# Smaller first transfers on two queues, GpSimd squares with a fold, and one load issued one tile earlier, in a hybrid decoder layer on one core

## The chip, the cores and the metric

The kernel runs on one core of a Trainium2 chip. The metric is the time of one execution on the device, in microseconds (us). The core has five engines that run side by side and wait for each other through semaphores: TensorE (PE; its weight loads are shown apart as PEld), VectorE (DVE), ScalarE (ACT), GpSimd (POOL) and SyncE (SP). SyncE here does nothing but issue transfers between the main memory and the on-chip memory (SBUF); ScalarE's queue may issue transfers too. TensorE writes to the accumulator banks (PSUM).

## What is computed

A decoder layer for 1024 tokens of width 1024 in float32. The change touches the first and the third of these steps:

```python
h = rmsnorm(x, ln1[l])
z = h @ w_in[l]
...
x = x + jnp.concatenate([ml_out, fx_out], axis=-1) @ w_out[l]
x = x + cross_attention(rmsnorm(x, ln_x[l]), rmsnorm(mem, ln_mem[l]), w_xq[l], w_xkv[l], w_xo[l])
u = jax.nn.relu(rmsnorm(x, ln2[l]) @ w_ff1[l])
x = x + (u * u) @ w_ff2[l]
return rmsnorm(x, ln_f)
```

Here `rmsnorm(x, g)` is `x * rsqrt(mean(x*x) + eps) * g` over the width, and between the second and third line stand an mLSTM group and a forgetting-attention group of heads, whose outputs are concatenated.

## The kernel before

**Layout.** Activations lie with the width on the 128 partitions: x is 8 tiles (k = 0 to 7) of 128 x 1024 tokens, kept as two halves (hf = 0, 1) of 512 tokens, `xs[hf][k]`, in the buffers `xa` and `xb`. Every matmul is done in three passes over operands split into a high part (`wh`, or `act` for activations) and a low part (`wl`): `mm3`, L184 to L186. `split` makes the two parts: ScalarE copies the high part (L132, or L135 with a scale), VectorE subtracts it to get the low part (L133, or L136 with a scale).

**The opening.** The first product is that of the mLSTM values with 16 gate columns beside them, 272 columns in all. L323 to L332 issue its transfers: for each k the tile of x (L319), for every even k the weights of two k (L326), and on ScalarE's queue the vector of gains and biases (`vec`, L329) and the gate weights (L330). In the block `with in_order()` (L377) the order of each compute engine is that of the program text: for each k the weights are split (`cut_w`), the gate weights of three k at k = 0, 2, 4 (`cut_gates`), the tile of x is scaled by its gain and split (`cut_x`), and twelve matmuls follow (`first_values`, four token tiles of three passes). A second loop does the same for hf = 1 with three token tiles. The normalisation is applied to the results, so the sum of squares is only needed then: `square_to` (L363) squares two tiles at once into `wide`, 128 x 1024 with tile k-1 in the left half and tile k in the right; `add_to` (L366) adds these on VectorE; `rsqrt_sums` (L238) sums over the partitions with matmuls against a column of ones, two parts (left and right) for each of four token tiles; L196, GpSimd's power (L202) and L207 to L209 turn the sums into the factors `rcol`, and `first_sink` uses them (L311, L375). The sums of hf = 0 are taken at k = 1 of the second loop, and the three VectorE operations that follow them stand in VectorE's order ahead of `cut_x(1, 6)`. The sums of hf = 1 come later, outside the block (L416).

**The rest of the order.** Outside such blocks a scheduler that models the engines orders the instructions, and transfers go out on SP's queue in its order.

**The second output projection.** The heads' outputs lie in main memory as `mix`. The projection is done in two parts; the second (`out_proj`, loop at L1069 over hf) takes its operands from `mix_load` (L845, two transfers of 768 KB for each hf, high and low part). Those for hf = 0 are loaded ahead of the loop, those for hf = 1 inside `full_sink` (L1073), held behind the store `done` (L1078) of one of the tiles n of hf = 0. `full_sink` loads the partial sum of the first projection (L1076), adds (L1077), stores, splits (L135, L136) and squares (L226, L230). The weights of this projection come by L172.

Of the kernel before, what the change touches and what calls it, by code (L numbers as in the profile page):

```python
# [11 lines left out]
AF = mybir.ActivationFunctionType  # L12
ALU = mybir.AluOpType
# [6 lines left out]
TH = 512  # L20
# [24 lines left out]
def hybrid_layer(ctx: ExitStack, tc: tile.TileContext, a: dict, out: bass.AP):  # L45
    nc = tc.nc
    v, s, g = nc.vector, nc.scalar, nc.gpsimd
# [7 lines left out]
    def name(tag):  # L55
        count[0] += 1
        return f"{tag}_{count[0]}"
# [4 lines left out]
    def act(dt=F32R):  # L62
        return sb("act", [P, 8, TH], 7, dt)
# [8 lines left out]
    def w4(shape=(P, 1024), dt=F32):  # L72
        t = sb("w4", [P, 1024], 5, dt)[: shape[0]]
        return t.rearrange("p (a b) -> p a b", b=shape[2]) if len(shape) == 3 else t

    def z4():
        return sb("z4", [P, T + 3], 2)

    def w2(tag, n=512, dt=F32, p=P):
        return sb("r_" + tag, [P, 512], BUFS[tag], dt)[:p, :n]  # L80
# [6 lines left out]
    def ps_tile(tag):  # L87
        return psum.tile([P, 512], F32, tag=tag, name=name(tag), bufs=PBUFS[tag])
# [19 lines left out]
    def const(n, shape, dt=F32):  # L108
        return pool.tile(shape, dt, tag=n, name=n, bufs=1)

    load = nc.sync.dma_start
# [29 lines left out]
    @contextmanager  # L141
    def in_order():

        traced = nc.cur_bb.bb.instructions
        last = traced[-1]
        yield
        start = next(k for k in reversed(range(len(traced))) if traced[k] is last) + 1
        for i in traced[start:]:
            if i.engine not in COMPUTE:
                continue  # L150
            if i.engine in last_of:
                tc.add_manual_dep(
                    i,
                    last_of[i.engine],
                    mybir.DependencyInfo(mybir.DependencyClass.NoSync, mybir.DependencyReason.DATA),
                    reason="in_order",
                )
            last_of[i.engine] = i.name


    def rotate(*tags):

        spare[tags] = spare.get(tags, -1) + 1
        return w2(tags[spare[tags] % len(tags)])
# [58 lines left out]
    def square_sum(acc, x, first, by=s, add=v):  # L223
        sq = acc if first else w2("c")[:, : x.shape[-1]]
        if by is s:
            s.activation(sq, x, AF.Square)  # L226
        else:
            by.tensor_tensor(out=sq, in0=x, in1=x, op=ALU.mult)
        if not first:
            add.tensor_tensor(out=acc, in0=sq, in1=acc, op=ALU.add)  # L230

    def rsqrt_sums(acc, r, nt, parts=1, bank=None, over=None, how=rsqrt_cols):

        ps = (bank or ov_)()
        for t in range(nt):
            for e in range(parts):
                at = (e * nt + t) * P
                nc.tensor.matmul(ps[:, t : t + 1], acc[:, at : at + P], ones, start=e == 0, stop=e == parts - 1)  # L238
        return how(r, ps[:, :nt], 1.0 / D, nt, over)
# [13 lines left out]
    rcol = const("rcol", [P, 8])  # L253
# [47 lines left out]
    xs = [[t[:, k] for k in range(KT)] for t in (xa, xb)]  # L301
# [11 lines left out]
    def load_x(hf, i):  # L313
        for k in range(4 * i, 4 * i + 4):
            load(xs[hf][k], a["x"][:, k, hf * TH : hf * TH + TH])
# [5 lines left out]
    raws = [sb("wr", [P, 1024], 2) for _ in range(2)]  # L321
    wg_raw = z4()[:, : KT * 16].rearrange("p (k c) -> p k c", k=KT)
    for k in range(KT):  # L323
        if k % 2 == 0:
            c = slice(k % 4 * 256, k % 4 * 256 + 512)
            load(raws[k // 4][:, c], a["w_mv"][0, k // 4, :, c])  # L326
        load_x(0, k)
        if k == 0:
            s.dma_start(vec, a["vec"])  # L329
            s.dma_start(wg_raw, a["w_gate"])  # L330
    for k in range(KT):
        load_x(1, k)  # L332

# [6 lines left out]
    def cut_x(hf, k, n=1):  # L340
        for c in range(0, TH, TH // n):
            c = slice(c, c + TH // n)
            split(h[hf][0][:, k, c], h[hf][1][:, k, c], xs[hf][k][:, c], vec[:, VEC["ln1"] + k :][:, 0:1])

    def first_values(hf, k, ts):
        w = both(ws[k // 3], lambda z: z[:, k % 3])
        for t in ts:
            mm3(tiles[hf][t], both(h[hf], lambda z: z[:, k, t * P : (t + 1) * P]), w, k == 0, k == KT - 1)

    def cut_w(k):  # L350
        w = both(ws[k // 3], lambda z: z[:, k % 3, :256])
        split(*w, raws[k // 4][:, k % 4 * 256 : k % 4 * 256 + 256])

    def cut_gates(i):
        w = both(ws[i], lambda z: z[:, :, 256:])
        split(*w, wg_raw[:, 3 * i : min(3 * i + 3, KT)])


    wide = [w4() for _ in range(3)]
    pairs_ = lambda hf, k: (xa, xb)[hf][:, k - 1 : k + 1].rearrange("p a b -> p (a b)")  # L360

    def square_to(t, hf, k):
        s.activation(t, pairs_(hf, k), AF.Square)  # L363

    def add_to(t, u):
        return v.tensor_tensor(out=t, in0=t, in1=u, op=ALU.add)  # L366
# [5 lines left out]
    def first_sink(hf, t):  # L372
        ps = tiles[hf][t]
        mv_sink(4 * hf + t, 0, ps[:, :256])
        v.tensor_scalar(out=z[:, 4 * hf + t], in0=ps[:, 256:], scalar1=rcol[:, 4 * hf + t : 4 * hf + t + 1], scalar2=None, op0=ALU.mult)  # L375

    with in_order():  # L377
        for k in range(KT):
            cut_w(k)
            if k in (0, 2, 4):  # L380
                cut_gates(k // 2)
            cut_x(0, k, 1 if k else 2)
            if k in (1, 3, 5):
                square_to(wide[k // 2], 0, k)
            if k == 4:
                add_to(wide[0], wide[1])
            first_values(0, k, range(4))
        square_to(wide[1], 0, 7)
        cut_x(1, 0)
        add_to(wide[0], wide[2])  # L390
        cut_x(1, 1)
        add_to(wide[0], wide[1])
        for k in range(2, 6):
            cut_x(1, k)
        for k in range(KT):
            if k in (2, 3):
                cut_x(1, k + 4)
            if k == 2:
                square_to(wide[1], 1, 1)
            if k == 4:  # L400
                square_to(wide[2], 1, 3)
            first_values(1, k, range(3))
            if k == 1:
                rsqrt_sums(wide[0], rcol[:, 0:4], 4, 2)
            if 2 < k < 7:
                first_sink(0, k - 3)
            if k == 6:
                add_to(wide[1], wide[2])
                square_to(wide[0], 1, 5)
        square_to(wide[2], 1, 7)  # L410
        add_to(wide[1], wide[0])
        last_sum = add_to(wide[1], wide[2])
    tiles[1].append(ps_tile("mm")[:, :WV])
    for k in range(KT):
        first_values(1, k, (3,))
    rsqrt_sums(wide[1], rcol[:, 4:8], 4, 2)  # L416
    for t in range(4):
        first_sink(1, t)

# [264 lines left out]
    for _ in range(2):  # L684
        t = act().rearrange("p a b -> p (a b)").rearrange("p (i c) -> p i c", i=4)
# [156 lines left out]
    def mix_load(k0, k1, hf):  # L842
        t = act().rearrange("p (e k) c -> p e k c", e=2)
        for p_ in range(2):
            load(t[:, p_, : k1 - k0].bitcast(F32), mix[hf, p_, :, k0:k1])  # L845
        return [(t[:, 0, k], t[:, 1, k]) for k in range(k1 - k0)]
# [204 lines left out]
    n = 0  # L1051
# [7 lines left out]
    for step in fill:  # L1059
        n, e = divmod(halves[0], 2)  # L1060
# [8 lines left out]
    for hf in range(2):  # L1069
        hi, lo = act(), act()  # L1070
        acc = w2("b")

        def full_sink(n, hf, ps):  # L1073
            t = rotate("p", "d", "e")
            with tc.issue_after(last_raw[0].ins):
                load(t, x1d[hf, :, n])  # L1076
            v.tensor_tensor(out=t, in0=ps, in1=t, op=ALU.add)  # L1077
            done = load(x1d[hf, :, n], t)  # L1078
            if hf == 0 and n == 1:
                with tc.issue_after(done.ins):  # L1080
                    mix_fx.append(mix_load(MLH + KX, KT, 1))
            split(hi[:, n], lo[:, n], t, vec[:, VEC["ln_x"] + n :][:, 0:1])
            square_sum(acc, t, n == 0)
            if hf == 1 and n == KT - 3:
                mix_done.append(done)
            if hf and n == 2:
                rsqrt_sums(acc0, rcol[:, 0:4], 4)
            if hf and n == 4:
                row_second(0)

        def row_second(hf):
            at = slice(hf * TH, hf * TH + TH)
            to_row(row[:, at], rcol[:, 4 * hf : 4 * hf + 4], 4, rowd[2:3, at])

        out_proj(a["w_out_b"], mix_fx[hf], hf, full_sink)
        h2.append((hi, lo))
        acc0 = acc
# [197 lines left out]
    for n in range(KT):  # L1295
# [7 lines left out]
        k = n % 4  # L1303
# [150 lines left out]
    for at, (p_, i) in enumerate(jobs):  # L1454
# [19 lines left out]
        b, k = todo[p_][:2]  # L1474
# [53 lines left out]
    for at, (b, m) in enumerate(steps):  # L1528
# [14 lines left out]
        x = x2[m // 2][:, m % 2]  # L1543
# [16 lines left out]
    for i in range(2):  # L1560
        t = act()
# [122 lines left out]
```

## Time and profile before

| | us |
|---|---|
| median of 3 runs | 1526.88 |
| lowest and highest | 1526.77, 1527.15 |
| the profiled execution, its own time | 1527.38 |
| its span, from the first to the last instruction | 1525.5 |
| TensorE busy in it | 1504.9 |
| VectorE busy | 1103.9 |
| ScalarE busy | 722.6 |
| GpSimd busy | 444.7 |
| first matmul begins | 6.46 |

The profile is one execution seen by the hardware profiler; times in it count from the first instruction. A row of the timeline has the start, the duration (of a group, from its first start to its last end), engine, line, operation, output and inputs by the program's names, shapes, count, and in brackets how long the engine stood idle before it and what ended that. A row of a group of instructions has, behind the count, the busy time and the mean duration in ns. Rows with "q" (SPq, ACTq) are instructions that issue transfers. A row "A <- B: total, times, longest" says how long A waited for B.

### The profile page before, as it was taken

The page shows a single profiled execution, that of the slowest core. Times are in us where ns is not written, and L with a number is a line of the kernel's source. Part 1 is how long each engine was busy: PE and PEld are TensorE (multiplying, and loading weights), DVE is VectorE, ACT ScalarE, POOL GpSimd, SP SyncE. Part 2 cuts the span into 40 slices and gives each one's busy share as a digit, 9 for nine tenths or more (in the row PEclk, how much of TensorE's full clock was granted, in tenths as well). Part 3 has the DMA queues.
Part 4 walks back from the last instruction along what each step waited for, and adds up shares of the span by engine and source line. Part 5 has one row for each costly group of instructions (what it writes and reads, how often), then busy time and mean ns, then how long its engine had stood idle before and what let it go on. Part 6 is the DMA issues. An engine that isn't in the chain of part 4 may idle for free.

```text
span 1525.5 us, 21947 instructions
## 1 busy us (share of the span) xinstructions
PE 1504.9 (99%) x7729; PEld 1261.5 (83%) x7729; DVE 1103.9 (72%) x1740; ACT 722.6 (47%) x1353; POOL 444.7 (29%) x498
## 2 busy tenths in 40 slices
PE   8999999999999999999999999999999999999997
PEld 8988888889899888788888888888888888888887
DVE  7675676764788885854557888887987788777765
ACT  7333343434688763644444456655566432222134
POOL 1003030413455441001100033433343644343312
PEclk9999999999999999999999999999999999999998
DMA  6232323435887957953334436777775975555623
GB/s 240 80 107 77 124 77 124 132 127 158 262 246 226 297 189 272 320 202 118 124 133 161 169 104 242 283 268 249 261 263 207 365 262 221 220 221 219 250 83 111
DMA packets 118075, 297.24 MB, mean 195 GB/s; under 512 B 13119, under 2 KB 27769, under 8 KB 111821
## 3 DMA queue, kind: packets, MB, share of 16 engines
q1 hardware_dynamic: 117676, 295.73, 56.4%
q8 instruction: 61, 1.00, 0.3%
q14 instruction: 50, 0.40, 0.1%
q10 hardware_dynamic: 288, 0.11, 0.0%
HBM read 199.08 MB, written 96.71 MB: 194 GB/s over the span
## 4 chain that ended last, share of the span: by engine, by line
PE 94%; DMA 2%; DVE 1%; ACT 1%; issue 1%; POOL 0%; SPq 0%; DVEq 0%; ACTq 0%; POOLq 0%
PE tp L184 8%; PE tp L186 8%; PE tp L185 8%; PE sc L184 6%; PE sc L186 6%; PE sc L185 6%; PE m L184 6%; PE mm L184 6%; PE m L186 6%; PE m L185 6%; PE mm L186 6%; PE mm L185 6%; PE ov L785 2%; PE ov L184 2%; PE ov L185 2%; PE ov L186 2%
## 5 line engine op out<-in xcount | busy, mean ns | idle before, releaser
L185 PE MATMUL tp<-act,wh 128*128 128x512 f32 (+1 forms) x456 | 178.7, 392 | 1.3 <-DMA act<-mix 1.3
L184 PE MATMUL tp<-act,wl 128*128 128x512 f32 (+1 forms) x456 | 179.2, 394 | 0.6 <-DVE wl L133 0.4
L186 PE MATMUL tp<-act,wh 128*128 128x512 f32 (+1 forms) x456 | 178.4, 392 | 0.0
L132 ACT ACTIVATE wh<-wr 128x1024 fp32r<-128x1024 f32 (+3 forms) x100 | 96.1, 962 | 107.6 <-PE tp L186 36.6
L133 DVE TENSOR_TENSOR wl<-wr,wh 128x1024 fp32r<-128x1024 f32 (+3 forms) x100 | 116.9, 1170 | 21.1 <-ACT wh L132 21.0
L184 PE MATMUL mm<-act,wl 128*128 128x512 f32 (+1 forms) x332 | 128.3, 386 | 0.0
L185 PE MATMUL mm<-act,wh 128*128 128x512 f32 (+1 forms) x332 | 126.9, 382 | 0.0
L186 PE MATMUL mm<-act,wh 128*128 128x512 f32 (+1 forms) x332 | 126.8, 382 | 0.0
L184 PE MATMUL m<-act,wl 128*128 128x512 f32 (+1 forms) x308 | 119.5, 388 | 0.0
L186 PE MATMUL m<-act,wh 128*128 128x512 f32 (+1 forms) x308 | 117.7, 382 | 0.0
L185 PE MATMUL m<-act,wh 128*128 128x512 f32 (+1 forms) x308 | 117.6, 382 | 0.0
L185 PEld LDWEIGHTS tp<-act,wh 128*128 128x128 f32 x456 | 85.8, 188 | 20.7 <-issue 1.6
L184 PEld LDWEIGHTS tp<-act,wl 128*128 128x128 f32 x456 | 85.8, 188 | 20.4 <-DVE wl L133 0.8
L186 PEld LDWEIGHTS tp<-act,wh 128*128 128x128 f32 x456 | 85.8, 188 | 19.6
L184 PE MATMUL sc<-act,wl 128*128 128x512 f32 (+1 forms) x260 | 100.8, 388 | 0.0
L185 PE MATMUL sc<-act,wh 128*128 128x512 f32 (+1 forms) x260 | 100.5, 387 | 0.0
L186 PE MATMUL sc<-act,wh 128*128 128x512 f32 (+1 forms) x260 | 100.5, 387 | 0.0
L1428 POOL TENSOR_TENSOR z<-wr 128x256 f32<-128x256 f32 x56 | 54.8, 998 | 143.6 <-DMA wr<-w_ff2q 130.3
L132 ACT ACTIVATE w<-wr 128x768 fp32r<-128x768 f32 (+2 forms) x31 | 25.5, 825 | 131.7 <-PE tp L186 69.6
L132 ACT ACTIVATE wh<-z 128x1024 fp32r<-128x1024 f32 (+2 forms) x55 | 52.5, 956 | 64.5 <-POOL z L1428 28.3
L133 DVE TENSOR_TENSOR wl<-z,wh 128x1024 fp32r<-128x1024 f32 (+2 forms) x55 | 68.2, 1240 | 9.9 <-ACT wh L132 9.9
L186 PEld LDWEIGHTS mm<-act,wh 128*128 128x128 f32 x332 | 62.4, 188 | 12.6
(657 smaller groups left out, 4205.7 us busy)
## 6 DMA issues: line engine op xcount, KB each, us to landing
act<-right SPq DMA_DIRECT2D x35, 1024.0 KB
right<-r_d SPq DMA_DIRECT2D x70, 256.0 KB
right<-w SPq DMA_DIRECT2D x56, 256.0 KB
wr<-w_ff2q SPq DMA_DIRECT2D x28, 512.0 KB
act<-fqk SPq DMA_DIRECT2D x48, 256.0 KB
wr<-w_in SPq DMA_DIRECT2D x20, 512.0 KB
wr<-w_ff SPq DMA_DIRECT2D x20, 512.0 KB
fqk<-r_p SPq DMA_DIRECT2D x32, 256.0 KB
```

The lines of the kernel that those rows point to most:

```text
L132: s.activation(hi, src, AF.Copy)
L133: return v.tensor_tensor(out=lo, in0=src, in1=hi.bitcast(F32), op=ALU.subtract)
L184: nc.tensor.matmul(ps, w[1], x[0], start=first, stop=False, skip_group_check=more)
L185: nc.tensor.matmul(ps, w[0], x[1], start=False, stop=False, skip_group_check=more)
L186: nc.tensor.matmul(ps, w[0], x[0], start=False, stop=last, skip_group_check=more)
L785: nc.tensor.matmul(self.ov[:, c0:], self.fv[:, self.j], t[:, c0:], start=self.j == 0 and t is self.p[1], stop=self.last and t is self.p[0])
L1428: g.tensor_tensor(out=o, in0=x, in1=y, op=op)
```

## The change

Three edits.

First, the opening's first transfers are cut into pieces of 128 KB: the weights of k = 0 and of k = 1 are loaded apart, the left half of x's first tile goes on ScalarE's queue in place of the gate weights, and SP issues the weights of k = 0, the gate weights, the right half of that tile, and then the rest as before.

Second, the squares of hf = 0 (four of 128 x 1024) are multiplications on GpSimd and no longer squares on ScalarE. After the last addition of each half GpSimd adds the right half of `wide` onto the left (`fold`, 128 x 512), and `rsqrt_sums` takes one part for each token tile where it took two.

Third, the load of the operands of hf = 1 stands behind the store of tile n = 0, where it stood behind that of n = 1.

```diff
     for k in range(KT):
-        if k % 2 == 0:
-            c = slice(k % 4 * 256, k % 4 * 256 + 512)
+        if k < 2 or k % 2 == 0:
+            c = slice(k % 4 * 256, k % 4 * 256 + (512 if k > 1 else 256))
             load(raws[k // 4][:, c], a["w_mv"][0, k // 4, :, c])
-        load_x(0, k)
-        if k == 0:
+        if k:
+            load_x(0, k)
+        else:
+
             s.dma_start(vec, a["vec"])
-            s.dma_start(wg_raw, a["w_gate"])
+            s.dma_start(xs[0][0][:, :256], a["x"][:, 0, :256])
+            load(wg_raw, a["w_gate"])
+            load(xs[0][0][:, 256:], a["x"][:, 0, 256:512])
...
     def square_to(t, hf, k):
-        s.activation(t, pairs_(hf, k), AF.Square)
+        x = pairs_(hf, k)
+        if hf:
+            s.activation(t, x, AF.Square)
+        else:
+            g.tensor_tensor(out=t, in0=x, in1=x, op=ALU.mult)
+
+    def fold(t):
+
+        g.tensor_tensor(out=t[:, :TH], in0=t[:, :TH], in1=t[:, TH:], op=ALU.add)
...
         add_to(wide[0], wide[1])
+        fold(wide[0])
...
-                rsqrt_sums(wide[0], rcol[:, 0:4], 4, 2)
+                rsqrt_sums(wide[0], rcol[:, 0:4], 4)
...
         last_sum = add_to(wide[1], wide[2])
+        fold(wide[1])
...
-    rsqrt_sums(wide[1], rcol[:, 4:8], 4, 2)
+    rsqrt_sums(wide[1], rcol[:, 4:8], 4)
...
-            if hf == 0 and n == 1:
+            if hf == 0 and n == 0:
                 with tc.issue_after(done.ins):
                     mix_fx.append(mix_load(MLH + KX, KT, 1))
```

GpSimd's order in the opening, from the setting up of constants on (`c_y` is the output of the power, L202; `w` are the buffers of `wide`). Before:

```order
L124 AFFINE_SELECT causal<-causal 128x128
L498 MEMSET z_71_788 128x3
L202 TENSOR_TENSOR c_y_320<-c_var_318,half 128x4
L440 MEMSET w_40_476 12x1024
L202 TENSOR_TENSOR c_y_439<-c_var_437,half 128x4
```

And of the change (its lines are 14 higher behind the new functions; L371 is the square, L375 the fold):

```order
L124 AFFINE_SELECT causal<-causal 128x128
L371 TENSOR_TENSOR w_25_134<-act_86 128x1024
L371 TENSOR_TENSOR w_26_135<-act_86 128x1024
L371 TENSOR_TENSOR w_27_136<-act_86 128x1024
L512 MEMSET z_71_784 128x3
L371 TENSOR_TENSOR w_26_135<-act_86 128x1024
L375 TENSOR_TENSOR w_25_134<-w_25_134 128x512
L202 TENSOR_TENSOR c_y_319<-c_var_317,half 128x4
L454 MEMSET w_40_472 12x1024
L375 TENSOR_TENSOR w_26_135<-w_26_135 128x512
L202 TENSOR_TENSOR c_y_435<-c_var_433,half 128x4
```

Four squares and a fold now stand ahead of the first power, and a second fold ahead of the second.

SP's queue at the second output projection: the stores of the tiles of hf = 0 (`x1d<-r_p`, `r_e`, `r_d`: the tiles n = 0, 2, 1 in the scheduler's order), the loads of partial sums (`<-x1d`) and the operands (`<-mix`). Before:

```order
L1076 DMA r_p_6950<-x1d 128x512
L1078 DMA x1d<-r_p_6886 128x512
L1078 DMA x1d<-r_e_6931 128x512
L1076 DMA r_p_7019<-x1d 128x512
L1078 DMA x1d<-r_d_6903 128x512
L845 DMA act_6907<-mix 128x1536 x2
L1078 DMA x1d<-r_p_6950 128x512
L1076 DMA r_e_7066<-x1d 128x512
L172 DMA wr_7092<-w_out_b 128x768
```

And of the change:

```order
L1090 DMA r_p_6946<-x1d 128x512
L1092 DMA x1d<-r_p_6882 128x512
L859 DMA act_6886<-mix 128x1536 x2
L1092 DMA x1d<-r_e_6927 128x512
L1090 DMA r_p_7015<-x1d 128x512
L1092 DMA x1d<-r_d_6902 128x512
L1092 DMA x1d<-r_p_6946 128x512
L172 DMA wr_7088<-w_out_b 128x768
L1090 DMA r_e_7062<-x1d 128x512
```

The two loads of operands stand three places further ahead, directly behind the store of tile 0, and two stores and one load now follow them.

## The prediction

> **What bounds the kernel now.** I read the page first, then the waits of TensorE, then the stretches in which it waits.
>
> ```profile
> span 1525.5 us, 21947 instructions
> PE 94%; DMA 2%; DVE 1%; ACT 1%; issue 1%; POOL 0%; SPq 0%; DVEq 0%; ACTq 0%; POOLq 0%
> ...
> PE mm L184 <- DVE act L136: 6.5, 1, 6.5
> PE tp L185 <- DMA act<-mix: 1.3, 1, 1.3
> PE tp L184 <- DVE wl L133: 0.4, 1, 0.4
> ```
>
> The chain that ended last is TensorE for 94% of the span, so only what makes TensorE wait, or takes an instruction from it, can change the time. The change works at two of its waits: the 6.5 us ahead of the first matmul, and the wait for `act<-mix` near 624 us. It also takes column sums from TensorE and gives GpSimd work in the opening. So I looked at the opening by stretches (columns: length, then busy time and count of PE, PEld, DVE, ACT, POOL, then clock, DMA share, GB/s).
>
> ```profile
> 6.46:10.70 4.24, 4.24 (x18) 4.24 (x19) 3.44 (x8) 4.24 (x9) 0.00 (x0) 1.00 1.01 383
> 10.70:16.00 5.30, 5.30 (x43) 5.30 (x43) 4.67 (x10) 5.30 (x12) 0.10 (x1) 1.00 1.05 392
> 16.00:20.00 4.00, 4.00 (x34) 4.00 (x33) 3.60 (x7) 4.00 (x7) 0.00 (x0) 1.00 1.05 399
> 20.00:25.00 5.00, 5.00 (x44) 5.00 (x43) 5.00 (x8) 5.00 (x10) 0.00 (x0) 1.00 0.43 161
> ```
>
> TensorE runs without a gap from 6.46 on: 18 matmuls in 4.24 us (0.236 each), then 43 in 5.30 (0.123). VectorE is nearly full beside it: 3.44 + 4.67 + 3.60 + 5.00 = 16.71 us busy of 18.54, so 1.83 us of it are free. GpSimd does nothing. The two engines meet at the seventh tile of the second half (k = 6), where VectorE's cut (L136) at 28.53 releases the matmul at 29.33, after a gap of about 0.2:
>
> ```profile
> 28.53 1.41 DVE L136 SCALAR_TENSOR_TENSOR act<-act,vec,act 128x512 fp32r<-128x512 f32 x2
> ...
> 28.99 0.29 PE L186 MATMUL sc<-wh,act 128*128 128x272 f32 x1
> 29.33 0.39 PE L184 MATMUL sc<-w,act 128*128 128x272 f32 x1
> ```
>
> So VectorE has no slack there: what delays it before 28.5 delays TensorE.
>
> **First transfers.** Before, SP issues 256 KB of weights and then 256 KB of x, and ScalarE the vectors and gate weights:
>
> ```profile
> 0.79 0.40 SPq L326 DMA_DIRECT2D wr<-w_mv  x1
> 1.20 0.45 ACTq L330 DMA_DIRECT2D z<-w_gate  x1
> 1.25 0.91 SPq L319 DMA_DIRECT2D act<-x  x2
> ...
> 4.47 0.42 ACT L132 ACTIVATE wh<-wr 128x256 fp32r<-128x256 f32 x1 [1.50 <-DMA wr<-w_mv]
> 5.38 0.91 ACT L135 ACTIVATE act<-act,vec 128x256 fp32r<-128x256 f32 x2 [0.15 <-DMA act<-x]
> ```
>
> The first matmul needs 128 KB of each; now only these stand ahead, on two queues, so 256 KB fewer. At the 383 GB/s of the second stretch that is 0.67 us; nothing at least, 1.0 at most if the weights' earlier arrival counts too. I take 0.7: first matmul near 5.7. The bytes up to x's second tile are the same, so that tile comes no sooner (an estimate: 5.38 plus 256 KB at 383 GB/s, so about 6.0).
>
> **Squares on GpSimd.** Four squares of 128x1024 leave ScalarE and become GpSimd operations with two SBUF inputs. No such size is in the trace. The nearest rows:
>
> ```profile
> L1172 POOL TENSOR_TENSOR r_e<-z,z 128x512 f32<-128x512 f32 x7 | 9.1, 1298 | 130.6 <-DMA z<-w_ff 127.9 <-DVE w L1172 2.7
> L230 POOL TENSOR_TENSOR r_b<-r_c,r_b 128x256 f32<-128x256 f32 x10 | 7.3, 734 | 32.7 <-ACT r_c L226 32.7
> L751 POOL TENSOR_SCALAR w<-w,c_den 128x512 f32<-128x512 f32 x8 | 5.5, 693 | 11.1 <-DVE c_den L748 5.3 <-ACT r_c L794 1.9 <-ACT wh L952 1.8
> ```
>
> 256 more elements cost 1.298 - 0.734 = 0.564 us, so 1024 take 1.298 + 2 x 0.564 = 2.43; I take 2.4. Upper end 2 x 1.298 = 2.6; lower end 2 x 0.693 = 1.39, if squaring one tensor reads it once, as the one-input form does. (The Trainium skill, GPSIMD Engine Reference, section 3.1, gives 4497 ns for an add of 2048 elements; halved, an estimate of 2.25, with which the sum below would be 0.7 us lower. No run here shows that size.)
>
> The price is not GpSimd's own time but VectorE's. Rows of both engines, elsewhere in the kernel:
>
> ```profile
> 906.10 1.30 POOL L1172 TENSOR_TENSOR z<-z,z 128x512 f32<-128x512 f32 x1
> 907.37 1.75 POOL L1172 TENSOR_TENSOR r_e<-wr,wr 128x512 f32<-128x512 f32 x1
> 909.20 2.16 POOL L1211 TENSOR_TENSOR wr<-wr 128x512 f32<-128x512 f32 x1
> ...
> 906.84 1.12 DVE L1172 TENSOR_TENSOR w<-r_f,r_p 128x512 f32<-128x512 f32 x1 [0.17 <-ACT r_f L1326]
> 907.88 2.32 DVE L133 TENSOR_TENSOR wl<-z,wh 128x1024 fp32r<-128x1024 f32 x1
> ...
> L505 DVE SCALAR_TENSOR_TENSOR z<-z,vec,z x24: 1270/1277/1857, 78.6 to 320.4; 128x1024 f32<-128x1024 f32 x24
> ...
> 18.09 1.22 DVE L366 TENSOR_TENSOR w<-w,w 128x1024 f32<-128x1024 f32 x1
> 19.23 0.74 DVE L136 SCALAR_TENSOR_TENSOR act<-act,vec,act 128x512 fp32r<-128x512 f32 x1
> ```
>
> L1172 on VectorE ends at 907.96, which is GpSimd's end (907.40) plus its own 0.6. GpSimd's next takes 1.75 instead of 1.30: it waited for that end. L133, begun at 907.88, takes 2.32 where 1.22 is usual, so it started at GpSimd's end, 909.12; GpSimd's next then takes 2.16. The two take turns, whole instructions at a time; the form with a scalar does so too (L505, 1.857 against 1.27). Every operation of VectorE in the opening has two SBUF inputs.
>
> I walk through the opening by turns, with VectorE's steps (start to start; its rows overlap by 0.08, as 18.09 + 1.22 and 19.23 show): an addition 1.14, a cut of 512 0.66, a weight split 0.34.
>
> ```profile
> 6.72 0.42 DVE L133 TENSOR_TENSOR wl<-wr,wh 128x256 fp32r<-128x256 f32 x1
> ...
> 21.03 2.73 DVE L136 SCALAR_TENSOR_TENSOR act<-act,vec,act 128x512 fp32r<-128x512 f32 x4
> ```
>
> The first square starts when x's second tile is there (6.0) and VectorE has ended its split of weight 1 (6.72 + 0.34 before, now 0.7 sooner), so at 6.3, and holds VectorE to 8.7. Cut 1 runs, 8.7 to 9.4. Tile 3, three loads of 256 KB behind tile 1, has meanwhile landed (6.0 + 3 x 0.67 = 8.0, the ninth microsecond at the latest): second square 9.4 to 11.8. One weight split, then the third square, 12.1 to 14.5. Only now comes cut 2 (14.6 to 15.3): TensorE, done with k=1 at 11.2, waits about 4.2 us. Weight splits and cuts 3 and 4 follow, then the addition of the first two squares; the fourth square needs that addition (18.9 to 21.3), and k=5 waits 2.2 us. Then the rest of VectorE's list, into which the fold puts one more turn (28.2 to 29.5, 1.3). The cut of 28.53 comes at 36.5: **8.0 us later**. Check by sums: 4 x 2.4 + 1.3 = 10.9 of turns, less the 1.83 free, less 0.7 that VectorE starts sooner, is 8.4. That ScalarE is rid of four squares is no gain: it was ahead of VectorE by then. The last wait before that cut is GpSimd's power (L202) behind the sums, as before. TensorE passes that point 8.0 us later, and the first transfers' 0.7 is spent in its waits. At 1.39 a square (and 0.69 the fold) the same count gives 4 x 1.39 + 0.69 - 1.83 - 0.7 = 3.7; at 2.6 it gives 9.2, 0.8 more.
>
> **Fewer sums.** The fold halves the column sums of L238:
>
> ```profile
> 40.84 1.84 PE L238 MATMUL ov<-ones,w 128*128 128x1 f32 x16
> 42.55 0.36 PE L184 MATMUL m<-wh,act 128*128 128x256 f32 x1
> ```
>
> Sixteen pass in 1.71 us, so eight save 0.86. The first set lies ahead of the late cut and saves nothing; the second saves 0.86. Its fold has cover: TensorE has matmuls of its list to do meanwhile, and the sums stand 13 of them later in the new order. Without cover it would cost its 1.3.
>
> **The second projection's operands.** They are issued at 617.88, behind the store of tile 1; now behind that of tile 0, whose store went out at 612.85, so about 4.6 us sooner.
>
> ```profile
> 612.85 0.39 SPq L1078 DMA_DIRECT2D x1d<-r_p  x1
> ...
> 617.88 1.10 SPq L845 DMA_DIRECT2D act<-mix  x2
> ...
> 623.30 0.39 PE L186 MATMUL m<-act,wh 128*128 128x512 f32 x1
> 623.94 0.47 PE L184 MATMUL tp<-act,wl 128*128 128x512 f32 x1 [0.25 <-DMA act<-mix]
> 625.75 0.47 PE L185 MATMUL tp<-act,wh 128*128 128x512 f32 x1 [1.34 <-DMA act<-mix]
> ...
> 629.56 0.39 PE L186 MATMUL mm<-act,wh 128*128 128x512 f32 x1
> 630.33 0.50 PE L184 MATMUL tp<-act,wl 128*128 128x512 f32 x1 [0.38 <-DVE wl L133]
> ```
>
> Matmuls of this size follow each other at 0.23, so L185 at 625.75 is 1.98 late (623.30 + 0.47 = 623.77) and 630.33 is 0.54 late. Landing took until about 625.7; 4.6 sooner is 621.1, well ahead of 623.5. The first 1.98 go. The 0.54 hang on weights queued behind the same 1.5 MB; I count half. Gain 2.25, between the 1.6 of the two named waits and 2.5. Stores and loads of two tiles (`x1d<-r_e`, `r_p<-x1d`) now stand behind the 1.5 MB, up to 4 us at 383 GB/s; the additions that use them feed banks that TensorE needs two tiles later, so I cost this at nothing, 0.5 if that cover is gone.
>
> **Sum**, against the profiled execution (1527.38 us, 0.50 above the median of 1526.88): 8.0 - 0.86 - 2.25 = +4.9, so 1532.3 there and **1531.8** as a median.
>
> **Rivals.**
>
> 1. The squares don't hold VectorE up. For it: L136 itself is never seen beside a reading GpSimd, and no row squares a tensor with itself. Against it: L133, L1172, L505 above. Then the change does what it says: 0.7 sooner, 0.86 twice, 2.25, and the 0.2 of the gap: -4.9, so 1522.0. It decides at once: cut 1 would end before 8 us.
> 2. A square costs the one-input price, 1.39. Opening +3.7, so 3.7 - 0.86 - 2.25 = +0.6, 1527.5. For it only that both inputs are one tensor.
> 3. TensorE falls back to its slow pace in the 4.2 us wait before k=2. The trace has the pace once, at the start: 18 matmuls at 0.236 where 0.123 is usual, 2.0 us lost. Here most of this would run out in the 2.2 us wait at k=5; if that wait is shorter, up to 2.0 more, 1533.8. The Trainium skill (TensorE: Matmul & The Clock Gate, Part 1) lets the clock fall to half after about one idle window of 3.4 us; by that rule the wait would suffice and the time be that of this rival, or the forecast's if the waits hide it. No wait of this length stands in the trace, which neither confirms nor denies it.
> 4. The change of order moves no DMA sooner: the operands stand in SP's new order directly behind tile 0's store, with no wait of their own, so I give this nothing apart from the bounds.
>
> **How the numbers follow.** Forecast 0.70, rival 1 0.12, rival 2 0.10, rival 3 0.08. The forecast's own range is 1530 to 1533.5: +0.8 for squares of 2.6, +0.65 for the operands' low gain, and as much below. The range goes down to just below rival 2, 1527.2, and up to 1535.2 (rival 3 with both of those); rival 1 and a rest above are left out. What a measurement of this kernel can tell is about 0.2%, 3.05 us: slower means over 1529.9, faster under 1523.8. Faster 0.12 (rival 1); same 0.17 (rival 2 and 0.07 of the forecast's lower edge); slower 0.71.
>
> **What would show it.** The first matmul near 5.7. GpSimd's four squares as rows of 2.4 or more, VectorE's L136 of tile 1 with a duration near 2 or more instead of 0.75, TensorE waiting for `DVE act L136` twice or more in the first 25 us with a sum of 7 to 10, and the seventh cut of the second half near 36.5. L238 in groups of 8. No wait of TensorE for `act<-mix` past 600. The prediction is wrong if L136 keeps its 0.75 beside the squares, or if a square takes under 1.6 us.

## The result, and the profile after

The changed kernel takes 1535.2 us in the median of four runs (1534.5 to 1538.0) against 1526.9: 1.0053 times the kernel before, 95% interval 1.0041 to 1.0064. The medians lie 8.3 us apart where 4.9 were forecast. Five more runs, with a median of 1533.5, beside nine of the kernel before (the last experiment), gave 1.0036 (1.0022 to 1.0050), 5.5 us by that ratio. Runs of one and the same kernel spread over several us with the granted clock (0.995 to 0.998), so small differences are read here from the traces, by when TensorE reaches the same matmul. The page of the changed kernel, the span and the chain that ended last:

```profile
span 1531.8 us, 21931 instructions
...
PE 92%; DMA 3%; DVE 2%; ACT 1%; issue 1%; POOL 0%; SPq 0%; DVEq 0%; ACTq 0%; POOLq 0%
```

VectorE and the transfers, 1% and 2% of the chain before, are now 2% and 3%. The waits of TensorE show where (total, times, longest):

```profile
PE mm L184 <- DVE act L136: 9.7, 4, 6.0
PE sc L184 <- DVE act L136: 2.0, 1, 2.0
PE ov L238 <- POOL w L375: 0.4, 1, 0.4
...
PE mm L184 <- DVE r_d L1091: 0.9, 1, 0.9
PE m L184 <- DVE r_d L1091: 0.6, 1, 0.6
```

The single wait of 6.5 us for a cut of x has become five, of 11.7 in all; the wait for `act<-mix` is gone; two waits for `r_d`, sums of the second output projection, are new. Matching the same matmul in the traces of both kernels gives a running account. The third column is the profiled execution of the changed kernel, the fourth that of its later runs (experiment 12):

| place (start before, us) | what lies there | later than before, us | later, second trace |
|---|---|---|---|
| 6.46 | first matmul | -0.49 | -0.97 |
| 29.33 | k = 6 of the second half | +6.39 | +5.87 |
| 57 | behind the second column sums | +5.88 | +5.37 |
| 622 | ahead of the second projection's operands | +5.95 | +4.35 |
| 627 to 631 | behind them, the lowest value | +3.31 | +2.29 |
| 662 | end of that projection | +5.56 | +5.59 |
| 1515 | last column sums | +5.87 | +5.76 |

So the opening costs the 6.4, the second sums return 0.5, and the sooner operands return 2.6 that are lost again within 35 us. In the second trace the opening costs 5.9, and the operands return 2.1 of which more than all, 3.3, is lost by 662. Between 57 and 622 us both traces go up and down by about 1 us at waits for ScalarE in stretches that the change doesn't touch. The rest of the 6.3 by which the span grew lies behind the last matmul and isn't explained.

**The opening.** GpSimd's squares (L371) and fold (L375), with VectorE beside them:

```profile
7.81 1.89 POOL L371 TENSOR_TENSOR w<-act 128x1024 f32<-128x1024 f32 x1 [6.03 <-DMA act<-x]
9.89 4.14 POOL L371 TENSOR_TENSOR w<-act 128x1024 f32<-128x1024 f32 x2 [0.19 <-DMA act<-x]
...
18.08 2.01 POOL L371 TENSOR_TENSOR w<-act 128x1024 f32<-128x1024 f32 x1 [1.72 <-DVE w L378]
26.31 1.73 POOL L375 TENSOR_TENSOR w<-w 128x512 f32<-128x512 f32 x1 [6.22 <-DVE w L378]
```

```profile
8.43 1.83 DVE L136 SCALAR_TENSOR_TENSOR act<-act,vec,act 128x512 fp32r<-128x512 f32 x1 [0.91 <-ACT act L135]
10.18 2.11 DVE L133 TENSOR_TENSOR wl<-wr,wh 128x256 fp32r<-128x256 f32 x1
12.21 1.89 DVE L133 TENSOR_TENSOR wl<-z,wh 128x48 fp32r<-128x48 f32 x1
14.03 0.74 DVE L136 SCALAR_TENSOR_TENSOR act<-act,vec,act 128x512 fp32r<-128x512 f32 x1
...
18.26 2.38 DVE L136 SCALAR_TENSOR_TENSOR act<-act,vec,act 128x512 fp32r<-128x512 f32 x1
...
26.15 3.77 DVE L136 SCALAR_TENSOR_TENSOR act<-act,vec,act 128x512 fp32r<-128x512 f32 x4
...
34.92 1.41 DVE L136 SCALAR_TENSOR_TENSOR act<-act,vec,act 128x512 fp32r<-128x512 f32 x2
```

Each square has one instruction of VectorE beside it that is too long. A cut takes 0.74 (14.03), but 1.83 and 2.38 at 8.43 and 18.26; a split of 128x256 takes 0.41, but 2.11; one of 128x48, which took 0.21, takes 1.89. These four are 1.1, 1.7, 1.7 and 1.6 longer than usual, and the fold puts 1.04 into the group of four cuts at 26.15 (2.73 before): 7.2 in all. The cut of k = 6 starts at 34.92 in place of 28.53, and TensorE stands before it:

```profile
35.72 0.40 PE L184 MATMUL sc<-w,act 128*128 128x272 f32 x1 [1.96 <-DVE act L136]
```

The squares come 1.5 later than the prediction had them because x's second tile does: GpSimd's first square needs only x's first two tiles and starts at 7.81 (7.32 in the second trace), and at 6.06 in experiment 2, which has the old transfers. SP's queue of the changed kernel, and ScalarE's rows that wait for what it brings:

```profile
0.79 0.41 SPq L326 DMA_DIRECT2D wr<-w_mv  x1
1.25 0.43 SPq L333 DMA_DIRECT2D z<-w_gate  x1
1.73 0.43 SPq L334 DMA_DIRECT2D act<-x  x1
2.21 0.43 SPq L326 DMA_DIRECT2D wr<-w_mv  x1
2.68 0.43 SPq L319 DMA_DIRECT2D act<-x  x1
```

```profile
6.64 0.42 ACT L132 ACTIVATE wh<-wr 128x256 fp32r<-128x256 f32 x1 [0.84 <-DMA wr<-w_mv]
7.67 0.72 ACT L135 ACTIVATE act<-act,vec 128x512 fp32r<-128x512 f32 x1 [0.61 <-DMA act<-x]
```

The second tile is the fifth transfer that SP issues, at 2.68; before it was the third, the second of the pair begun at 1.25. Each issue takes 0.43 and the next follows at 0.47. ScalarE scales the tile at 7.67 in place of 6.50. Fewer bytes have moved, too. The transfers of the first 7 us, in the kernel before and in the changed one:

```profile
DMA packets 1012, 1.44 MB, mean 206 GB/s; under 512 B 234, under 2 KB 362, under 8 KB 1012
```

```profile
DMA packets 1142, 1.15 MB, mean 164 GB/s; under 512 B 251, under 2 KB 891, under 8 KB 1142
```

The smaller pieces go as smaller packets, and 1.15 MB pass in place of 1.44. So the tile is late by its later issue, by the slower transfers, or by both; no experiment parts the two.

**The second projection.** SP's waits for stores to land in this stretch (611 to 662 us), in the kernel before and in the changed one:

```profile
SPq L1076 <- DMA x1d<-r_p: 8.9, 4, 3.2
...
SPq L1076 <- DMA x1d<-r_e: 2.8, 2, 2.0
```

```profile
SPq L1090 <- DMA x1d<-r_e: 11.0, 3, 4.6
SPq L1090 <- DMA x1d<-r_p: 4.7, 4, 2.2
```

With those for `r_d` (2.1 and 0.7) they make 13.8 us before and 16.4 in the change.

SP's rows in the changed kernel:

```profile
618.66 0.96 SPq L859 DMA_DIRECT2D act<-mix  x2
619.73 0.53 SPq L1092 DMA_DIRECT2D x1d<-r_e  x1
...
623.70 0.45 SPq L172 DMA_DIRECT2D wr<-w_out_b  x1
628.85 0.32 SPq L1090 DMA_DIRECT2D r_e<-x1d  x1
```

The store of `r_e` goes out right behind the 1.5 MB. The next load into `r_e` has to wait until that store has landed, and goes out 9.1 us after it (628.85 less 619.73). Before, it went out 6.3 us after the store (619.55 less 613.29) and without a wait. SP stands at that load for 4.6 us, and everything behind it in the queue stands with it, again twice later. The partial sums come late, VectorE's additions with them, and TensorE waits for `r_d`.

### The profile page after: what moved, and what is told of

It is laid out like the page before. It is cut to its first block, busy times and chain, and to the rows that moved or that the text cites. A ratio compares the mean times of both kernels' runs of the same rounds, so it can differ in the third digit from the quotient of the medians.

```text
span 1531.8 us, 21931 instructions
## 1 busy us (share of the span) xinstructions
PE 1504.5 (98%) x7713; PEld 1259.5 (82%) x7713; DVE 1106.9 (72%) x1740; ACT 721.6 (47%) x1349; POOL 453.2 (30%) x504
## 4 chain that ended last, share of the span: by engine, by line
PE 92%; DMA 3%; DVE 2%; ACT 1%; issue 1%; POOL 0%; SPq 0%; DVEq 0%; ACTq 0%; POOLq 0%
PE tp L184 8%; PE tp L186 8%; PE tp L185 8%; PE sc L184 6%; PE sc L186 6%; PE sc L185 6%; PE m L184 6%; PE m L186 6%; PE mm L184 6%; PE m L185 6%; PE mm L186 6%; PE mm L185 6%; PE ov L184 2%; PE ov L185 2%; PE ov L799 2%; PE ov L186 2%
## 5 line engine op out<-in xcount | busy, mean ns | idle before, releaser
L184 PEld LDWEIGHTS mm<-act,wl 128*128 128x128 f32 x332 | 62.6, 188 | 13.1 <-DVE r_d L1091 1.3
```

What stands on the lines that cost most here:

```text
L184: nc.tensor.matmul(ps, w[1], x[0], start=first, stop=False, skip_group_check=more)
```

## The experiments

All but the last change one thing at a time, or put parts together. "Later at k = 6" and "later at the end" (the last column sums, at 1515) are against the trace of the kernel before. Four kernels whose opening is that of the kernel before up to k = 6 (experiments 5, 6, 8 and 9) differ there by +0.27, -0.13, +0.21 and +0.68, which is how finely this can be read.

| kernel | later at k = 6 | later at the end | ratio to the kernel before |
|---|---|---|---|
| change, squares on ScalarE | +2.02 | +1.97 | 1.0008 (0.9999 to 1.0017) |
| before, squares alone | +4.46 | +4.62 | 1.0024 (1.0015 to 1.0032) |
| before, folds alone | +1.06 | +1.05 | 1.0004 (0.9996 to 1.0013) |
| before, first transfers alone | +0.77 | +1.09 | 1.0004 (0.9996 to 1.0013) |
| before, one-input operation for the squares | +1.60 | +0.96 | 1.0005 (0.9997 to 1.0014) |
| before, second fold alone | +0.21 | -0.68 | 0.9998 (0.9989 to 1.0007) |
| before, operands alone | +0.27 | -0.25 | 0.9992 (0.9984 to 1.0001) |
| before, operands in two steps | -0.13 | -2.94 | 0.9986 (0.9977 to 0.9994) |
| the same, and second fold | +0.68 | -2.28 | 0.9987 (0.9979 to 0.9996) |
| the same, and x's first tile in halves | +1.21 | -1.45 | 0.9991 (0.9983 to 1.0000) |
| change, operands in two steps | +5.90 | +6.97 | 1.0028 (1.0020 to 1.0037) |
| change again | +5.87 | +5.76 | 1.0036 (1.0022 to 1.0050) |

**1. The change with the squares back on ScalarE.**

```diff
-        x = pairs_(hf, k)
-        if hf:
-            s.activation(t, x, AF.Square)
-        else:
-            g.tensor_tensor(out=t, in0=x, in1=x, op=ALU.mult)
+        s.activation(t, pairs_(hf, k), AF.Square)
```

> The changed kernel with one thing undone: the four squares of the first half of x are ScalarE's again; both folds, the first transfers and the sooner operands stay. Theory A (the squares hold VectorE up by turns): the seventh matmul group of the second half (k = 6), at 35.7 us in the changed kernel, comes back by 4 to 6.5 us, to between 29.3 and 31.7 (the first fold may still take a turn of 1.3), and the time falls from 1535.2 to between 1528.5 and 1531. Rival B (the opening is late because x's second tile now lands at 7.67 instead of 6.50, behind the smaller transfers): that landing stays, k = 6 stays above 33 and the time above 1533.

k = 6 stands at 31.35, 4.4 sooner than in the change. Theory A holds; rival B falls, though 2.0 of delay stay. Of these the first fold accounts for 1.06 (experiment 3), which leaves 0.96 to the first transfers.

**2. The squares alone**, put into the kernel before (the edit of experiment 1 backwards).

> The kernel before with one thing done: the four squares of the first half on GpSimd; no fold, no new transfers, operands as before. Theory A: four turns of 1.8 to 2.0 us each are 7.2 to 8.0, less the 1.83 that VectorE has free: k = 6 moves from 29.33 to between 34.5 and 35.5, and the time to 1532 to 1533. Rival B: the squares cost little by themselves, k = 6 below 31, time below 1529.

+4.46, just under the range: the squares are most of the loss by themselves. VectorE's excess is four times 1.64 to 1.70, 6.6 in all; less the 1.83 that it had free, 4.8. Here TensorE met a wait of 1.95 us ahead of k = 2 with its fast pace already reached. The stretches behind (length, then busy time and count of PE and PEld, DVE, ACT, POOL, then the granted clock):

```profile
11.92:13.93 2.01, 0.06 (x2) 0.01 (x1) 2.01 (x2) 1.94 (x5) 1.40 (x1) 1.00 1.05 389
13.93:17.56 3.63, 3.63 (x16) 3.63 (x17) 3.63 (x8) 3.63 (x7) 0.48 (x2) 0.53 1.06 387
17.56:20.00 2.44, 2.44 (x22) 2.44 (x21) 2.44 (x2) 1.81 (x4) 1.64 (x1) 1.00 0.85 330
```

For 3.63 us the clock is 0.53 and 16 matmuls pass, at 0.227 each. That is 1.7 us lost, but TensorE still waits 0.5 for k = 6 afterwards: VectorE sets that point, and the slow pace lies inside its delay.

**3. The folds alone.**

```diff
+        g.tensor_tensor(out=t[:, :TH], in0=t[:, :TH], in1=t[:, TH:], op=ALU.add)
...
+        fold(wide[0])
...
-                rsqrt_sums(wide[0], rcol[:, 0:4], 4, 2)
+                rsqrt_sums(wide[0], rcol[:, 0:4], 4)
...
+        fold(wide[1])
...
-    rsqrt_sums(wide[1], rcol[:, 4:8], 4, 2)
+    rsqrt_sums(wide[1], rcol[:, 4:8], 4)
```

> The kernel before with one thing done: both folds by GpSimd, with half as many column sums. Theory A: the first fold takes one turn of 1.3 us from VectorE, of which its free time covers at least part: k = 6 between 29.3 and 30.6; the second saves about 0.5 behind that (as in the changed kernel, where the gap of both kernels goes from 6.39 to 5.88 us there). Time between 1526.2 and 1527.7. Rival: folds are free and both sets of sums are saved in full, 2 x 0.86: 1525.2.

As the theory had it at k = 6 (+1.06) and behind the second sums (+0.55, so 0.51 back). Three cuts beside the fold:

```profile
21.03 3.11 DVE L136 SCALAR_TENSOR_TENSOR act<-act,vec,act 128x512 fp32r<-128x512 f32 x3
```

They take 3.11 where steps of 0.66 and a last 0.74 make 2.06: the fold's turn costs 1.05, the whole delay of k = 6. At the end the kernel is 1.05 later and not 0.55; the difference arises past 400 us, at waits for ScalarE.

**4. A GpSimd operation that reads one input**, in place of the squares, which it doesn't compute:

```diff
-        s.activation(t, pairs_(hf, k), AF.Square)
+        x = pairs_(hf, k)
+        if hf:
+            s.activation(t, x, AF.Square)
+        else:
+            g.tensor_scalar(out=t, in0=x, scalar1=0.0, scalar2=None, op0=ALU.max)
```

> The kernel before with the four squares of the first half replaced by a GpSimd operation of the same size that reads its input once (the maximum with 0, so the sums of squares of that half are not computed). It tells whether it is the reading of two SBUF inputs that makes GpSimd and VectorE take turns. Theory A1 (only GpSimd's operations with two SBUF inputs hold VectorE): VectorE's cuts keep their 0.75 us beside these, k = 6 stays within 0.5 of 29.3, time within 0.6 of 1526.9. Theory A2 (any GpSimd operation that reads SBUF holds VectorE's two-input ones): four turns of 1.39 less the free 1.83 are 3.7: k = 6 near 33, time near 1530.6.

+1.60: neither. GpSimd's third of these, and VectorE's rows beside it:

```profile
12.81 4.45 POOL L367 TENSOR_SCALAR w<-act 128x1024 f32<-128x1024 f32 x1
```

```profile
13.08 1.21 DVE L370 TENSOR_TENSOR w<-w,w 128x1024 f32<-128x1024 f32 x1
14.21 0.41 DVE L133 TENSOR_TENSOR wl<-wr,wh 128x256 fp32r<-128x256 f32 x1
14.55 1.52 DVE L136 SCALAR_TENSOR_TENSOR act<-act,vec,act 128x512 fp32r<-128x512 f32 x1
15.99 0.41 DVE L133 TENSOR_TENSOR z<-wr,w 128x256 fp32r<-128x256 f32 x1
```

The one-input operation stretches to 4.45 us while VectorE's instructions pass at their usual durations, all but one, which is held for 0.8 (1.52 in place of 0.74). The other three have one such instruction each, too; the four are 0.78 to 0.84 longer than usual, 3.2 in all. Less the free 1.83 that is 1.4, near the delay seen. So this form also takes something from VectorE, but half as much for each instruction. The squares kept VectorE out for 1.7 us of the 1.9 to 2.1 that they ran.

**5. The operands alone**, behind tile 0 (the change's own line, in the kernel before).

> The kernel before with one thing done: the operands of the second half of the second output projection are loaded behind the store of tile 0. Theory C (given back): TensorE's wait for `act<-mix` goes (about 2 to 2.6 us gained near 624 us), and within 30 us new waits on the additions of the partial sums (L1077, `r_d`, `r_p`, `r_e`) take 1.5 to 2.5 us of it back, because their loads, stores and the weights `w_out_b` stand behind the 1.5 MB: time between 1526.0 and 1526.9 against 1526.9 of the kernel before, span 0 to 0.8 lower. Rival D (the give-back in the changed kernel came from the late opening or from chance, not from the order of the transfers): 2.0 or more stays, span 1523.5 or less.

Theory C: 2.6 us gained from 621 to 631 (TensorE from 0.30 to 2.89 sooner), 2.5 lost again by 662 (0.42 sooner), with waits for `r_d` of 0.9 and 0.4 and SP standing 10.5 us at `r_e` here too. The opening has no part in it. Rival D falls.

**6. The operands in two steps**, the high part behind tile 0 and the low part behind tile 1 (`mix_load` takes the parts to be loaded as its last argument):

```diff
-            if hf == 0 and n == 1:
+            if hf == 0 and n < 2:
                 with tc.issue_after(done.ins):
-                    mix_fx.append(mix_load(MLH + KX, KT, 1))
+                    if n == 0:
+                        mix_hi.append(mix_load(MLH + KX, KT, 1, None, [0]))
+                    else:
+                        mix_fx.append(mix_load(MLH + KX, KT, 1, mix_hi[0], [1]))
```

> The kernel before with the operands of the second half loaded in two steps: the high part (768 KB) behind the store of tile 0, the low part behind that of tile 1. Theory C: the low part lands about 2 us sooner than in the kernel before, because the high part has gone ahead of it, so the wait of about 2 us for `act<-mix` goes; and what is queued behind either part waits for 768 KB (2 us) and not for 1.5 MB, so that the give-back is under 1 us: span 1.0 to 2.2 lower than the kernel before, below that of the whole operands behind tile 0. Rival: the give-back is the same, since the same bytes pass in the same 10 us: span within 0.5 of that kernel's.

Better than expected: 2.7 us gained in the stretch, and none given back (2.89 sooner at 632, 2.88 at 659). SP's longest waits there:

```profile
SPq L1080 <- DMA x1d<-r_p: 6.0, 5, 2.3
SPq L248 <- ACT row L247: 5.0, 1, 5.0
```

Its wait for the store of `r_e` is down to 1.1, and its waits for stores make 10.1 us in all, where the operands alone (experiment 5) made 17.8. The second of these rows is at the end of the projection, when the transfers are out. This is the one single part that beats the kernel before, by 2.1 us in the ratio.

**7. The first transfers alone.**

> The kernel before with one thing done: the first transfers in pieces of 128 KB on two queues. Theory A: the first matmul begins 0.5 to 0.9 sooner, x's second tile lands up to 1.2 later (as at 7.67 in the changed kernel against 6.50), VectorE has free time for it, and k = 6 (29.33 before) moves by 0 to +1.0; time 1526.9 to 1527.9. Rival: the sooner start comes through and the time falls by 0.5 to 0.9, to about 1526.2.

Theory A, but at its upper end: the first matmul at 5.47, 0.99 sooner, and k = 6 0.77 later. ScalarE scales x's second tile at 7.26 and has waited for the weights of k = 1 and then for the tile (1.1 and 0.4 us). One kernel with the old transfers stood 0.68 later at k = 6, so the 0.77 alone would not be clear of chance; the 0.96 left in experiment 1 points the same way. With what runs 2 and 3 gave, 4.46 + 1.06 + 0.77 = 6.29, the 6.39 of the whole opening (5.87 in the second trace) is accounted for.

**8. The second fold alone.**

> The kernel before with one thing done: the second of the two folds, with half as many column sums in the second set. Theory A: only the first fold costs a turn that TensorE feels (k = 6 was 1.06 later with both folds); here k = 6 stays at 29.3, and the sums give 0.5: TensorE 0.5 sooner from 45 us on, time 1526.4. Rival: the second fold, too, takes turns from VectorE where TensorE needs it, and nothing is gained: TensorE between 0.2 sooner and 1 later at 60 us.

From k = 6 to 60 us TensorE gains 0.50 (+0.21 to -0.29). The halved sums give 0.9, and some 0.4 is gone at 55 us, half of it a new wait for VectorE's `w` (L441, 0.22). Theory A in size; the ratio can't tell it from nothing.

**9. Both gains together.**

> The kernel before with the two single edits that gained: the operands in two steps (high part behind tile 0, low part behind tile 1; alone 2.9 us in the trace, ratio 0.9986) and the second fold with its halved sums (alone 0.5 at 60 us). If the gains add, as they lie 580 us apart: TensorE 0.3 to 0.6 sooner at 60 us and 3.2 to 3.6 sooner behind 660 us, span 1521 to 1522.5, ratio 0.9976 to 0.9985. Rival: the gain of the two steps was one run's chance (the same stretch moved by 0.4 to 1.6 us between kernels that don't touch it): less than 2.0 behind 660 us.

The two steps hold: 2.6 gained again (+0.07 at 622, -2.62 at 632). The fold's 0.9 from k = 6 to 53 us (+0.68 to -0.22) shrinks to 0.5 by 58, and this run's opening happened to be 0.7 later. The ratio is that of the two steps alone; a gain of the second fold on top isn't shown.

**10. The change with its operands in two steps.**

> The changed kernel with its operands in two steps in place of both behind tile 0. If the give-back of the changed kernel comes from the 1.5 MB in one piece, the opening stays (+5.9 at 60 us against the kernel before) and the stretch from 610 to 660 us gains 2.3 to 2.9 where it gained 0.16: span 1528.8 to 1529.5, time 1531.5 to 1533. Rival (the give-back comes from the late opening): span within 0.7 of 1531.8.

The span is 1532.4, the rival's figure, but some 1.5 us of it come from TensorE's clock. TensorE waits 1.96 us for k = 6, as in the change, and then (columns as in experiment 2):

```profile
35.23:36.71 1.48, 1.48 (x11) 1.48 (x12) 1.43 (x4) 1.48 (x4) 0.00 (x0) 1.00 0.36 137
36.71:40.25 3.54, 3.54 (x19) 3.54 (x17) 3.54 (x9) 2.19 (x5) 0.00 (x0) 0.52 0.21 74
```

The same wait, also of 1.96 us, in the changed kernel was followed by none of this, nor was it in the second trace:

```profile
35.72:40.00 4.28, 4.28 (x34) 4.28 (x35) 4.23 (x11) 3.48 (x7) 0.00 (x0) 1.00 0.28 99
```

So TensorE, 5.90 later than before at k = 6, is 6.93 later at 57 us, where the second sums should have brought it to 5.4. In the stretch itself the result lies between the two: 2.2 gained by 632 (+6.98 to +4.74), 1.3 to 1.5 given back by 662. The ratio is lower than the change's first, but its interval overlaps that of the change's later runs. That one piece of 1.5 MB costs more than two of half the size is shown by runs 5 and 6 side by side; why the two steps give back something in the changed kernel and nothing in the kernel before stays open (SP stood 5.2 us at `r_e` here).

**11. x's first tile in halves on two queues**, without the two further issues on SP:

```diff
             s.dma_start(vec, a["vec"])
+            s.dma_start(xs[0][0][:, :256], a["x"][:, 0, :256])
+            load(xs[0][0][:, 256:], a["x"][:, 0, 256:512])
             s.dma_start(wg_raw, a["w_gate"])
```

> The kernel with both gaining edits, and x's first tile in two halves on two queues, with the weights of k = 0 and 1 still in one transfer and the gate weights on ScalarE's queue behind the half of x. Theory A (what made x's second tile late was that SP issues the gate weights and the weights of k = 1 ahead of it, two issues of 0.47 us): here SP issues that tile where the kernel before does, near 1.7 us, so ScalarE scales it at 6.5 (and not at 7.3 to 7.7), the first matmul begins 0.1 to 0.5 sooner than 6.46, and k = 6 (29.33) is not later than 29.6: time within 0.5 of the kernel without this edit. Rival: the gate weights, one issue later, hold the first matmul: it begins at 6.5 or later.

The rival: the gate weights, now third on ScalarE's queue, come late,

```profile
6.46 0.24 ACT L132 ACTIVATE wh<-z 128x48 fp32r<-128x48 f32 x1 [1.62 <-DMA z<-w_gate]
```

and ScalarE, whose order is fixed here, stands 1.62 us before them. The first matmul begins at 7.67. This says nothing against the smaller pieces themselves: the gate weights held ScalarE, and whether the tile was there at 6.5 can't be seen. In the first 7 us 1.58 MB moved, more than the 1.44 before, with x's first tile in two pieces and the weights in one.

**12. The change again.**

> The changed kernel itself, in more runs beside the kernel before on one chip. Theory: what the trace accounts for is +5.9 to +6.3 us (6.4 in the opening, 0.5 back with the second sums, 0.2 back with the operands), and the 8.3 between the two medians holds some 2 us that come from the granted clock of single runs (0.995 to 0.998) and from few runs: ratio 1.0033 to 1.0043, 1532.5 to 1534 against 1527.5. Rival: a cost that the profiled execution does not show: ratio 1.005 or more again. In the trace: k = 6 at 35.2 to 36.4 us, and of the 2 to 2.9 us gained at `act<-mix` at most 1 left behind 660 us.

1.0036 and the last column of the first table: the theory. Of the gain at `act<-mix` nothing is left behind 660 us. A median of 8.3 us above the kernel before was at the high end of what this kernel does; the intervals, 1.0041 to 1.0064 and 1.0022 to 1.0050, overlap.

## Why the prediction was right, point by point

**Direction and main mechanism: right.** VectorE was the bound of the opening, GpSimd's squares shut it out whole instructions at a time, and k = 6 came late by that (experiments 1 and 2). Rival 1 (squares don't hold VectorE) and rival 2 (a square at the one-input price, +3.7 in the opening) fall by the rows at 8.43 to 18.26. Of the signs named, the long cut of the second tile (1.83), the sums in groups of eight, k = 6 near 36.5 (35.72) and no wait for `act<-mix` came. Squares of 2.4 did not (1.89 to 2.07), and the waits before k = 2 and k = 5, forecast as 4.2 and 2.2, were three of 1.1 to 1.4.

**The square, 2.4, was too dear.** The squares' rows are 1.89 to 2.07 long, near the middle of the bounds 1.39 and 2.6. A whole turn costs VectorE 1.7, and the four turns and the fold of the changed kernel add up to 7.2, not 10.9. The prediction leaned on the slope of two-input rows at other lines. The estimate from the figure of the Trainium skill (GPSIMD Engine Reference, section 3.1) was 2.25, nearer, and also above.

**"The bytes up to x's second tile are the same, so that tile comes no sooner": this is the step that failed.** It counted bytes, but neither issues nor the rate at which the pieces pass. Two more issues on SP stand ahead of that tile, which was issued 1 us later and scaled 1.2 later than before; in the five traces with the new transfers it was scaled at 7.03 to 7.67, in the eight with the old ones at 6.20 to 6.51 (experiment 11, where the gate weights held ScalarE, aside). The 6.0 forecast for its landing is what experiment 2 shows with the old transfers (6.06). How much is due to the issues and how much to the rate (1.15 MB in 7 us in place of 1.44) stays open. The prediction let VectorE start 0.7 sooner; in experiment 7 k = 6 is 0.77 later with the smaller transfers. The two errors of the opening have opposite signs: 7.2 of turns, less 1.83 free, plus 0.77 is 6.1, against 8.0 forecast and 6.4 measured.

**Second column sums, 0.86 forecast, 0.5 kept.** The sums themselves gave about 0.9 (experiment 8); the rest went to what VectorE and TensorE meet 10 us later.

**Operands, 2.25 forecast, 2.6 gained and 2.5 given back** (2.1 and 3.3 in the second trace). The gain at the wait was right, in the first trace with the 0.54 counted in full. The step that failed is the cost of nothing, at most 0.5, for the stores and loads behind the 1.5 MB. It looked at the banks that TensorE needs two tiles later and not at the queue: a store that lands late keeps SP at the next load into the same buffer, and with it all that SP is yet to issue.

**Rival 3 (slow pace after a wait)** did not come in the two traces of the change, whose waits between 9 and 21 us were 1.1 to 1.4 long and not 4.2. It came in experiment 2 after 1.95 us, in experiment 1 after 0.84 and 0.9 of column sums (0.51 from 25.1 to 28.6 us) and in experiment 10 after 1.96. The rule cited from the Trainium skill (TensorE: Matmul & The Clock Gate, Part 1) has the clock fall after about one idle window of 3.4 us; the trace of experiment 2 shows a fall to 0.53 after less, for 3.6 us. As 1.96 us were followed by a fall in experiment 10 and by none in the change, the length of a wait alone does not decide it here. The price lay inside the delay of VectorE in experiments 1 and 2, as the forecast had it; in experiment 10 some 1.5 us of it stayed.

**The sum.** 6.4 - 0.5 - 0.1 against 8.0 - 0.86 - 2.25: the opening was too dear by 1.6 and the two gains behind it too large by 2.5, which together make 5.8 (5.9 in the trace) in place of 4.9. That errors of opposite sign left only 1 us is luck. The first runs' median of 1535.2 stands at the very end of the stated range, 1527.2 to 1535.2, and above the forecast's own, 1530 to 1533.5; that of the later runs, 1533.5, stands at the end of the second.

## What to carry to other kernels

Before work is given to an idle GpSimd, ask whether VectorE beside it is nearly full and reads two tensors in SBUF: a two-input GpSimd instruction of 1.9 us cost VectorE 1.7 here, and relieving an engine that was not the bound buys nothing. When a load is moved forward or cut into pieces, count the issues on its queue and look for the next instruction there that waits for a store to land: a large load in front of such a store holds up the whole queue, and the same load in two steps kept 2.3 to 2.9 us in experiments 6 and 9 (0.7 to 1.0 behind the late opening of experiment 10), where one piece kept 0.4 at most.

## What was not expected of the hardware

- A GpSimd operation with one input of 128x1024 took up to 4.45 us beside VectorE's two-input instructions and held VectorE for only 0.8; with two inputs it took 1.9 to 2.1 and held VectorE for 1.7.
- TensorE's clock fell to 0.51 to 0.53 for some 3.5 us in three traces, behind waits of 0.84, 1.95 and 1.96 us. Behind another wait of 1.96 us, at the same matmul of the changed kernel, it stayed at 1.00.
- With two further issues on SP ahead of a tile, 0.47 us each, and smaller pieces, the tile was usable 0.5 to 1.2 us later than in the kernel before, although no bytes were added ahead of it.
